# A Hymba-style decoder layer: part of the weight sums of its seven-product cells made by accumulating DMAs, and four more such cells

## The chip, the cores and the metric

The kernel runs on one core of a Trainium2 chip. A core has the matrix engine TensorE (PE; its weight loads are listed as PEld), VectorE (DVE), ScalarE (ACT), GpSimd (POOL) and SyncE (SP, which here only issues DMAs), and 16 DMA engines. The metric is the device time of one execution in microseconds (us), the median of several runs.

## The reference

One layer over 256 tokens with a model width of 2048, all in float32: RMSNorm and one input projection; a Mamba-2 style SSD scan and a sliding-window attention side by side; one output projection; a feed-forward block with a causal convolution over three tokens; and a gate that adds a per-layer embedding. The change lies in the last two parts:

```python
u = _rmsnorm(h, ffn_norm_g[i]) @ w_up[i]               # 2048 -> 2 * 5632
u = _causal_dwconv(u, ffn_conv_w[i], ffn_conv_b[i])
g_ff, u_ff = jnp.split(u, [D_FF], axis=-1)
h = h + (jax.nn.silu(g_ff) * u_ff) @ w_down[i]         # 5632 -> 2048
gate = jax.nn.sigmoid(_rmsnorm(h, ple_norm_g[i]) @ w_ple_gate[i])
pe = _rmsnorm(p[i] @ w_ple_proj[i], ple_post_g[i])
h = h + gate * pe
```

## The kernel before

**Products.** Each float32 operand is split into a rounded high part and a low part (`wh` by a cast on ACT, `wl` by a subtraction on DVE; the same for the left sides: `ah`, `al`, `ph`, `pl`, `gh`, `gl`). A product of a 128x128 block with a 128x512 block is three matmuls: high by high, high by low, low by high. They add up in one of eight PSUM banks. A weight load by SP brings 128 x 1024 values (512 KB), two blocks of 128x512; ACT casts the whole of it in one step and DVE subtracts the whole of it in one step.

**Cells.** The up projection runs over 11 pairs of columns `c` (512 gate columns and 512 value columns, loads `wg` and `wu`) and in each over eight slices of 256 input features, `kp`. One `kp` of one `c` is a cell: a 2x2 block matrix (two halves of the tokens, two halves of the features) by a 2x2 block matrix (two halves of the features, gate and value columns). A plain cell makes eight products. A mixed cell makes seven, after Winograd's form of Strassen's scheme: the left side is kept with four sums of its blocks (S1 to S4, made once, `left`), and on the weights' side four sums must be made anew in each cell. In `cell_mixed` they are a0, a1 (into a tile `ta`), b0 and b1 (written over `wg`), each a 128x512 step on DVE; then `ta` and the new `wg` are split like loaded weights, and the value half `wu[1]` is split by itself (`vh`, `vl`). A mixed cell's products go to banks P1, P6, P7, P5, which hold only mixed products and are combined by `sums` when the last mixed cell is through, and to Q2, Q4, Q3, Q22.

Which `kp` can be mixed is `MIXED`; which are, in a given `c`, is `FEWER`; the order of the cells is `BEGIN` for c = 0 and `STEADY` after it. The gate projection has the same cells in two passes (`GATES`, `GATES_SECOND`). There are 43 mixed cells: 2, 3, 3 in c = 0, 1, 2, four in each of c = 3 to 8, three in each of c = 9 and 10, and 3 + 2 in the gate passes.

**Stages.** After `up(c)` come the transposes, convolution and gating of its result (`gated`, which leaves `gh` and `gl` in one of `GBUF` buffers) and, from c = 2 on, two of the four output blocks of the down projection of the pairs finished before (`down`; four weight loads for each output block, two for each of the two pairs' `g`). The first output block's banks are P1 and P6 of the up stage just ended, the second's P7 and P5.

**Order.** Tiles are allocated in rings; a plan (`Plan`) holds every step with its engine, an assumed duration, what it follows and which ring slots it takes. PE's order is as written; the other engines' orders come from a list schedule by latest starts, in which `hop` is the time from one engine to another (0.15 us) and `lag` the time that a DMA needs beyond its issue. `QUEUE` is added to a hop in the first estimate of the latest starts. Each engine then works through its own list in order. Loads have a ring of `WR` = 7 raw buffers, splits a ring of `WB` + 1 = 5 pairs. For the two stages before (SSD and attention) `Recorder`, a subclass, does the same and may reorder PE too; it plans each of the two stages.

POOL does little in these stages: a power for each reciprocal root (line 664). It issues no DMA anywhere in the kernel.

Names that a reader of the profile meets: line 341 is the helper that all steps of the SSD and attention stages go through; 1511 and 1515 are the split of weights (ACT, DVE); 1557 to 1559 the three matmuls of a product; 1731 the sums b0 and b1, 1754 the sums a0 and a1, 1739 and 1743 the split of `vh`, `vl`; 1793 the sums out of the banks (`c<-c,b`); 1903 and 1907 the split of the gated block; 2104 to 2115 the gate's last steps and 2153 the last matmuls, of half width.

Of the kernel before, what the change touches and what calls it, by code (L numbers as in the profile page):

```python
# [21 lines left out]
P = 128  # L22
# [21 lines left out]
MIXED = (1, 3, 5, 7)  # L44
BEGIN = [0, 2, 4, 6, 1, 3, 5, 7]
STEADY = [0, 1, 2, 3, 5, 4, 7, 6]
FEWER = {0: (1, 3), 1: (1, 3, 5), 2: (1, 3, 5), 9: (1, 3, 5), 10: (1, 3, 5)}
GATES = (1, 3, 5)
GATE_FIRST = [0, 2, 1, 3, 4, 6, 5, 7]
GATES_SECOND = (3, 5)  # L50
AHEAD = 3
LEFT_DMA = (3,)
GATE_DMA = (1, 2)
QUEUE = 1.0
ROUNDS = 6
GBUF = 3
TAPS = (0,)
TURNED = ("xb", "xb", "xb", "xb")
KEYS_DMA = (True, True)
# [234 lines left out]
class Recorder(Plan):  # L294
# [29 lines left out]
    def keep(self, real, shape, pool=None, tag=None, n=1, at=-20.0, dtype=F32):  # L324
        t = Lazy(shape, dtype, None, real=real)
        t.at = at
        if pool is not None:
            t.slot = self.ring(pool, tag, n).take()
        return View.whole(t)

    def group(self, extra=0.0):
# [195 lines left out]
def hybrid_layer(  # L527
# [283 lines left out]
    rx = sb(const, [P, NB], "rx")  # L811
    dtT = sb(small, [64, T], "hsq")
    acc_b, acc_c = acc_pair(), acc_pair()
# [83 lines left out]
    def squares(ss, n):  # L897

        for b in range(NB):
            sq = sb(small, [P, NC], "hsq")  # L900
            S.activation(out=sq, in_=hres[b][:, n * NC : (n + 1) * NC], func=AF.Square, accum_out=ss[:, b, n : n + 1])
# [22 lines left out]
    with tc.tile_pool(name="ssd", bufs=1) as sp, tc.tile_pool(name="dram", bufs=1, space=bass.MemoryType.DRAM) as dp:  # L924
# [14 lines left out]
        dt_ps = plan.keep(dt_ps, [P, NC], ps_ms, "ms", 2, -5.0)  # L939
        dtT = plan.keep(dtT, [64, T], small, "hsq", 2)  # L940
        real_h, hres = hres, [plan.keep(t, [P, D]) for t in hres]
# [285 lines left out]
    with tc.tile_pool(name="att_s", bufs=2) as as_, tc.tile_pool(name="att", bufs=2, reuse_waits="tile") as ap_, tc.tile_pool(name="ps_sc", bufs=1, space=PSUM) as ps_sc:  # L1227
# [33 lines left out]
        def norm_rope(acc, b, rope, gain=None):  # L1261
            r = sb(ap_, [P, NC], "qkr")
            S.activation(out=r, in_=acc[b], func=AF.Copy, scale=rx[:, b : b + 1])
            n = sb(small, [P, NC], "hsq")
            S.activation(out=n, in_=r, func=AF.Square)
# [202 lines left out]
    pe_d = scratch.tile([NB, P, D], F32, tag="pe_d", name="pe_d")  # L1468
    by_hand = tc.manual_schedule(engines={PE.engine, S.engine, V.engine, nc.sync.engine})
    by_hand.__enter__()  # L1470

    with tc.tile_pool(name="ffn", bufs=2, reuse_waits="tile") as fp:

        plan = Plan(before.rest)
        UNIT = 0.2275
        raws = Ring(WR, [2.7 * i - 15.0 for i in range(WR)])
        splits = Ring(WB + 1, [-8.1, -5.4, -2.7, 0.0, 0.0])
        rings = {}
# [12 lines left out]
        def load(src):  # L1491
            o = Box()
            o.slot = raws.take()

            def go():
                o.t = load_raw(src)

            o.job = plan.add("SP", 2.0, go, slots=[o.slot], lag=2.2)
            return o

        def split_weights(src, after, slot):
            o = Box()
            o.slot = splits.take()
            pool = fp if o.slot[1] % (WB + 1) == WB else wp

            def tile_(t):
                return sb(pool, [P, KW, NC], t, F32R, 1 if pool is fp else None)

            def hi():
                o.h = tile_("wh")  # L1510
                S.copy(o.h, src.t)  # L1511

            def lo():
                o.l = tile_("wl")
                V.tensor_tensor(out=o.l, in0=src.t, in1=o.h.bitcast(F32), op=ALU.subtract)  # L1515

            a = plan.add("ACT", 1.0, hi, after, [o.slot])
            b = plan.add("DVE", 1.17, lo, [a, *after])
            free(slot, a, b)
            o.jobs = [a, b]  # L1520
            return o
# [146 lines left out]
        def left(o, kp, source, gains_, tiles):  # L1668
# [35 lines left out]
            prev = ins  # L1704
            for q, x0, x1, op in ((3, 7, 2, ALU.add), (4, 3, 0, ALU.subtract), (5, 0, 7, ALU.subtract), (6, 1, 4, ALU.subtract)):
                prev = [
                    plan.add("DVE", 0.22, lambda q=q, x0=x0, x1=x1, op=op: V.tensor_tensor(out=F.t[:, q, :], in0=F.t[:, x0, :], in1=F.t[:, x1, :], op=op), prev)
                ]
# [16 lines left out]

        def cell_mixed(acc, L, src):

            wg, wu = (load(x) for x in src)

            def into(x, i, y, j, z, k, op, after):  # L1730
                return plan.add("DVE", 0.61, lambda: V.tensor_tensor(out=x.t[:, i], in0=y.t[:, j], in1=z.t[:, k], op=op), after)

            g = split_weights(wg, [wg.job], wg.slot)
            v = Box()
            v.slot = ring("v")

            def v_hi():
                v.h = sb(fp, [P, NC], "vh", F32R, 1)
                S.copy(v.h, wu.t[:, 1])

            def v_lo():
                v.l = sb(fp, [P, NC], "vl", F32R, 1)
                V.tensor_tensor(out=v.l, in0=wu.t[:, 1], in1=v.h.bitcast(F32), op=ALU.subtract)

            vh = plan.add("ACT", 0.55, v_hi, [wu.job], [v.slot])
            vl = plan.add("DVE", 0.61, v_lo, [vh, wu.job])
            ta = Box()
            ta.slot = ring("ta")

            def sums(i, j, y, k):  # L1750

                def go():
                    t = alloc(ta, "t", lambda: sb(fp, [P, KW, NC], "ta", bufs=1))
                    V.tensor_tensor(out=t[:, i], in0=wu.t[:, j], in1=y.t[:, k], op=ALU.subtract)

                return plan.add("DVE", 0.61, go, [wu.job, y.job], [ta.slot])

            a0 = sums(0, 0, wg, 0)
            a1 = sums(1, 1, wu, 0)
            a = split_weights(ta, [a0, a1], ta.slot)  # L1760
            b0 = into(wg, 0, wu, 1, ta, 0, ALU.subtract, [a0, *g.jobs])
            b1 = into(wg, 1, wg, 1, wg, 0, ALU.subtract, [b0])
            b = split_weights(wg, [b0, b1], wg.slot)
            free(wu.slot, a0, a1, vh, vl, b0)
            free(ta.slot, b0)
            def at(f):
                return lambda: (L.h[:, f, :], L.l[:, f, :])

            ups = [(P1, A11, g, 0), (Q2, A12, g, 1), (Q3, S4, v, None), (P5, S1, a, 0), (P7, S3, a, 1), (P6, S2, b, 0), (Q4, A22, b, 1)]
            for o, jobs, n in ((g, g.jobs, 2), (v, [vh, vl], 1), (a, a.jobs, 2), (b, b.jobs, 2)):  # L1770
                parts = [
                    (acc[m], at(f), (lambda: (v.h, v.l)) if i is None else pick(o, i)) for m, f, x, i in ups if x is o
                ]
                free(o.slot, multiply(parts, jobs + L.jobs))

        def cell_plain(acc, L, src):

            for x, out_ in zip(src, ((Q2, Q4), (Q3, Q22))):
                w = weights(x)
                free(w.slot, multiply([(acc[m], block(L, i, b), pick(w, i)) for b, m in enumerate(out_) for i in range(KW)], w.jobs + L.jobs))  # L1780

        def sums(acc):
# [3 lines left out]
            u2 = sum_(x, c0, acc[P6], [j])  # L1786
            j1 = sum_(y, x, acc[P5], [u2])
            j2 = sum_(x, x, acc[P7], [u2, j1])
            j3 = sum_(z, x, acc[P5], [j2])
            return (c0, Q2, [j, u2]), (x, Q4, [j2, j3]), (y, Q3, [j1]), (z, Q22, [j3])  # L1790

        def sum_(out_, x, bank_, after=()):
            job = plan.add("DVE", 0.61, lambda: V.tensor_tensor(out=out_(), in0=x(), in1=bank_(), op=ALU.add), [bank_.last, *after], [out_.slot])
            free(bank_.slot, job)
# [120 lines left out]
        def up(c, at, order, mixed, before=None):  # L1915

            acc = accumulators(at, len(mixed))
            for n, kp in enumerate(order):
                if before:
                    before(n)  # L1920
                (cell_mixed if kp in mixed else cell_plain)(acc, lefts[kp], (w_up[c, kp], w_up[NPAIR + c, kp]))
                if n == max(order.index(m) for m in mixed):
                    rest = sums(acc)
# [27 lines left out]
        def square(ss, n, b, after=(), at=-20.0):  # L1951

            def go():
                sq = sb(small, [P, NC], "hsq")
                S.activation(out=sq, in_=hres[b][:, n * NC : (n + 1) * NC], func=AF.Square, accum_out=ss[:, b, n : n + 1])
# [106 lines left out]
        for n in range(4):  # L2062
            for b in range(NB):
# [6 lines left out]
                def square_pe(o=o, n=n, b=b):  # L2070
                    t = sb(small, [P, NC], "hsq")
                    S.activation(out=t, in_=o.t, func=AF.Square, accum_out=ssp[:, b, n : n + 1])
# [46 lines left out]
        def gate(first, at, order, mixed):  # L2119
            acc = accumulators(at, len(mixed))  # L2120
            last = order[-2:] if first else []
            if first:
                acc[Q22].left -= KW
            for n, kp in enumerate(order):
                if not first and n == 1:
                    if 3 not in GATE_DMA:
                        turn_h(3, (2, 3))
                if kp in last:
                    continue
                (cell_mixed if kp in mixed else cell_plain)(acc, gates[kp], (w_pg[first, kp], w_pg[first + 1, kp]))  # L2130
                if mixed and n == max(order.index(m) for m in mixed):
                    rest = sums(acc)
# [99 lines left out]
```

## Time and profile before

| | us |
|---|---|
| median of 3 runs | 1386.26 |
| lowest, highest | 1384.36, 1388.0 |
| the profiled execution's own time | 1385.08 |
| its span, from the first to the last instruction's end with its DMA | 1383.3 |

In the profile, busy times are sums over the span; a row of a group gives the line, the engine, the operation, what it writes and reads with the shapes, the count, then the busy time and the mean length in ns of one, then the engine's idle time just before them and what ended it. A row of the timeline gives the start, the length and the instruction. Lengths overlap: an engine starts a step before the one ahead of it has quite ended, so what a step costs an engine is the distance of two starts.

### The profile page before, as it was taken

Reading aid. Unit: us, or ns where it says so; the run is one execution under the profiler, and the core shown is the slowest. Engines: PE = TensorE matmul, PEld = TensorE weight load, DVE = VectorE, ACT = ScalarE, POOL = GpSimd, SP = SyncE. Lnnn points to the kernel's source line nnn. Section 1 sums busy time; section 2 is a strip of 40 time slices with the busy share of each in tenths; the row PEclk is TensorE's granted clock in tenths of the full one; section 3 lists DMA queues with packets and bytes.
Section 4 is the critical chain, followed back from the end, with each engine's and each line's share of the span. In section 5 each row is a group of like instructions: output and inputs, shape, how many; then the busy total and the mean of one; then the engine's idle time right before and its main releaser. Section 6 shows DMA issues by size and latency. Waiting matters only on the chain.

```text
span 1383.3 us, 18291 instructions
## 1 busy us (share of the span) xinstructions
PE 1374.8 (99%) x6302; PEld 1124.4 (81%) x6302; DVE 1208.3 (87%) x1581; ACT 1045.7 (76%) x1414; POOL 131.8 (10%) x113
## 2 busy tenths in 40 slices
PE   9999999999999999999999999999999999999998
PEld 7888888888777778888888888888888888888886
DVE  5788787776789898699999999999899999977998
ACT  6699988754677766587997896878688687867963
POOL 0001010037055421000000000000000000000000
PEclk9999999999999999999999999999999999999999
DMA  9888879868698778596868868686777678688762
GB/s 336 272 238 250 224 218 248 215 183 245 181 228 202 215 213 210 189 243 214 245 203 233 229 187 245 211 238 206 219 224 218 209 208 251 189 254 258 210 222 92
DMA packets 204220, 306.81 MB, mean 222 GB/s; under 512 B 129376, under 2 KB 134112, under 8 KB 203872
## 3 DMA queue, kind: packets, MB, share of 16 engines
q1 hardware_dynamic: 203696, 305.18, 76.2%
q8 instruction: 49, 0.80, 0.3%
q10 hardware_dynamic: 432, 0.48, 0.1%
q14 instruction: 43, 0.35, 0.1%
HBM read 271.46 MB, written 4.26 MB: 199 GB/s over the span
## 4 chain that ended last, share of the span: by engine, by line
PE 94%; DVE 3%; ACT 2%; issue 1%; DMA 0%; SPq 0%; DVEq 0%; ACTq 0%
PE acc L341 32%; PE b L1557 18%; PE b L1559 18%; PE b L1558 18%; PE acc L825 3%; PE ms L341 1%; PE sc L341 1%; DVE wl L1515 1%; PE tr L341 1%; ACT wh L341 1%; DMA seg<-scr 0%; PE ms L630 0%; DVE c L2115 0%; DVE c L2114 0%; PE b L1657 0%
## 5 line engine op out<-in xcount | busy, mean ns | idle before, releaser
L1511 ACT CAST wh<-w 128x1024 fp32r<-128x1024 f32 x296 | 308.3, 1051 | 128.5 <-PE b L1559 89.4
L1515 DVE TENSOR_TENSOR wl<-w,wh 128x1024 fp32r<-128x1024 f32 x296 | 355.9, 1220 | 38.1 <-ACT wh L1511 37.1
L341 DVE TENSOR_TENSOR wl<-w,wh 128x1024 fp32r<-128x1024 f32 x180 | 236.0, 1317 | 74.8 <-ACT wh L341 70.4
L341 ACT CAST wh<-w 128x1024 fp32r<-128x1024 f32 x180 | 188.1, 1049 | 128.1 <-PE acc L341 113.1
L341 PE MATMUL acc<-wh,ah 128*128 128x512 f32 x448 | 176.7, 394 | 0.0
L341 PE MATMUL acc<-wh,al 128*128 128x512 f32 x448 | 174.6, 390 | 0.0
L341 PE MATMUL acc<-wl,ah 128*128 128x512 f32 x448 | 174.4, 389 | 0.0
L1557 PE MATMUL b<-wh,gh 128*128 128x512 f32 x398 | 154.9, 389 | 0.0
L1559 PE MATMUL b<-wh,gl 128*128 128x512 f32 x398 | 154.8, 389 | 0.0
L1558 PE MATMUL b<-wl,gh 128*128 128x512 f32 x398 | 154.8, 389 | 0.0
L1559 PE MATMUL b<-wh,al 128*128 128x512 f32 x362 | 140.9, 389 | 0.0
L1557 PE MATMUL b<-wh,ph 128*128 128x512 f32 x352 | 137.1, 390 | 0.0
L1559 PE MATMUL b<-wh,pl 128*128 128x512 f32 x352 | 137.0, 389 | 0.0
L1558 PE MATMUL b<-wl,ph 128*128 128x512 f32 x352 | 136.9, 389 | 0.0
L1557 PE MATMUL b<-wh,ah 128*128 128x512 f32 x346 | 134.7, 389 | 0.0
L1558 PE MATMUL b<-wl,ah 128*128 128x512 f32 x346 | 134.7, 389 | 0.0
L341 PE MATMUL acc<-wh,yh 128*128 128x512 f32 x256 | 101.5, 396 | 0.0
L341 PE MATMUL acc<-wl,yh 128*128 128x512 f32 x256 | 99.8, 390 | 0.0
L341 PE MATMUL acc<-wh,yl 128*128 128x512 f32 x256 | 99.7, 389 | 0.0
L341 PEld LDWEIGHTS acc<-wh,ah 128*128 128x128 f32 x448 | 84.1, 188 | 18.7 <-issue 1.4
L341 PEld LDWEIGHTS acc<-wh,al 128*128 128x128 f32 x448 | 84.1, 188 | 17.7
L341 PEld LDWEIGHTS acc<-wl,ah 128*128 128x128 f32 x448 | 84.1, 188 | 17.1 <-issue 0.2
(292 smaller groups left out, 2518.3 us busy)
## 6 DMA issues: line engine op xcount, KB each, us to landing
w<-in_w_up_dram SPq DMA_DIRECT2D x176, 512.0 KB, 4.3
w<-in_w_in_dram SPq DMA_DIRECT2D x126, 512.0 KB, 4.3
w<-in_w_down_dram SPq DMA_DIRECT2D x88, 512.0 KB, 4.3
w<-in_w_out_dram SPq DMA_DIRECT2D x64, 512.0 KB, 4.4
w<-in_w_pg_dram SPq DMA_DIRECT2D x32, 512.0 KB, 4.2
seg<-scr SPq DMA_DIRECT2D x8, 512.0 KB, 5.3
xt<-in_xT_dram SPq DMA_DIRECT2D x16, 128.0 KB, 6.8
h<-in_x_dram SPq DMA_DIRECT2D x2, 1024.0 KB, 8.6
```

The source lines that it names most:

```text
L341: getattr(real, method)(*(concrete(a) for a in args), **{k: concrete(a) for k, a in kw.items()})
L825: PE.matmul(acc[b], lhsT=aT(k, b)[part % 2], rhs=wt[:, c, :], start=(k == 0 and not part), stop=(k == KT - 1 and part == 2))
L1511: S.copy(o.h, src.t)
L1515: V.tensor_tensor(out=o.l, in0=src.t, in1=o.h.bitcast(F32), op=ALU.subtract)
L1557: PE.matmul(t, lhsT=hi, rhs=wh, start=first, stop=False)
L1558: PE.matmul(t, lhsT=hi, rhs=wl, start=False, stop=False)
L1559: PE.matmul(t, lhsT=lo, rhs=wh, start=False, stop=last)
```

## The change

- Two of a mixed cell's four weight sums, a1 and b1, are made by DMAs issued on POOL that add a 128x512 block of SBUF (256 KB) onto another, in all cells but those of c = 0, and in the gate passes. For that the signs of left blocks and sums are turned so that all four weight sums are additions; `sums` subtracts in two places instead. The planner books 1.4 us on POOL and a lag of 3.4 us for such a DMA. POOL's order in these stages now comes from the plan too.
- What is split changes with it: a0 alone gets a narrow split (`vh`, `vl`), and the whole of `wu`, once a1 is added onto its first half, a wide one. A cell still has three wide and one narrow split.
- A mixed cell's last product pair (b) is put on PE's list after the first products of the next cell (`Between`, `later`, `DELAY`), and `sums` comes one cell later.
- Four more cells are mixed: one each in c = 1, 9 and 10, and one in the second gate pass; 47 in all. `STEADY` and `BEGIN` are reordered.
- One more raw buffer (`MORE`), one more split pair (`PAIRS`); `GBUF` goes from 3 to 2, the scratch tile `hsq` from two buffers to one, and `ta` is half as wide.
- In `Recorder`, a hop from another engine to PE counts 1 us more (`MARGIN`), so the SSD and the attention stage are planned anew; `QUEUE` goes from 1.0 to 0.5.

```diff
-BEGIN = [0, 2, 4, 6, 1, 3, 5, 7]
-STEADY = [0, 1, 2, 3, 5, 4, 7, 6]
-FEWER = {0: (1, 3), 1: (1, 3, 5), 2: (1, 3, 5), 9: (1, 3, 5), 10: (1, 3, 5)}
+BEGIN = [0, 2, 4, 1, 6, 3, 5, 7]
+STEADY = [1, 2, 0, 3, 5, 4, 7, 6]
+FEWER = {0: (1, 3), 1: (1, 3, 5, 7), 2: (1, 3, 5)}
-GATES_SECOND = (3, 5)
+GATES_SECOND = (1, 3, 5)
-QUEUE = 1.0
+QUEUE = 0.5
+MARGIN = 1.0
-GBUF = 3
+GBUF = 2
+BY_DMA = (('a1', 'b1'),)
+GATE_BY_DMA = ("a1", "b1")
+ADD_LAG = 3.4
+DELAY = 1
+MORE = 1
+PAIRS = 2
+TWICE = 1
...
+    def hop(self, a, b):
+        return super().hop(a, b) + (MARGIN if b.engine == "PE" and a.engine != "PE" else 0.0)
...
-            sq = sb(small, [P, NC], "hsq")
+            sq = sb(small, [P, NC], "hsq", bufs=1)
...
-        raws = Ring(WR, [2.7 * i - 15.0 for i in range(WR)])
-        splits = Ring(WB + 1, [-8.1, -5.4, -2.7, 0.0, 0.0])
+        raws = Ring(WR + MORE, [2.7 * i - 15.0 for i in range(WR + MORE)])
+        splits = Ring(WB + PAIRS, [-8.1, -5.4, -2.7, 0.0, *[0.0] * PAIRS])
...
+            def onto(name, x, i, y, k, after):
+                def go():
+                    if name in by_dma:
+                        G.dma_start(out=x.t[:, i], in_=y.t[:, k], accum_op=ALU.add)
+                    else:
+                        V.tensor_tensor(out=x.t[:, i], in0=x.t[:, i], in1=y.t[:, k], op=ALU.add)
+                if name in by_dma:
+                    return plan.add("POOL", 1.4, go, after, lag=ADD_LAG)
+                return plan.add("DVE", 0.61, go, after)
...
+            a0 = plan.add("DVE", 0.61, first, [wu.job, wg.job], [ta.slot])      # ta = wu[0] + wg[0]
+            ah = plan.add("ACT", 0.55, a_hi, [a0], [a.slot])
+            al = plan.add("DVE", 0.61, a_lo, [ah])
+            a1 = onto("a1", wu, 0, wu, 1, [a0])
...
+                b0 = plan.add(
+                    "DVE", 0.61, lambda: V.tensor_tensor(out=wg.t[:, 0], in0=wu.t[:, 1], in1=ta.t, op=ALU.add), [a0, *g.jobs]
+                )
+            b1 = onto("b1", wg, 1, wg, 0, [b0])
...
+            def later():
+                b = split_weights(wg, [b0, b1], wg.slot)
+                product(b, [(P6, S2, 0), (Q4, A22, 1)])
+
+            product(g, [(P1, A11, 0), (Q2, A12, 1)])
+            between()
+            product(a, [(P5, S1, None)])
+            v = split_weights(wu, [a1], wu.slot)
+            product(v, [(P7, S3, 0), (Q3, S4, 1)])
+            return later
...
-                if n == max(order.index(m) for m in mixed):
+                if n == len(order) - 1 or not DELAY:
+                    between()
+                if n == min(max(order.index(m) for m in mixed) + DELAY, len(order) - 1):
                     rest = sums(acc)
```

More of the change, by code (lines that the diff above doesn't have):

```diff
@@ L811, in hybrid_layer @@
     rx = sb(const, [P, NB], "rx")
-    dtT = sb(small, [64, T], "hsq")
+    dtT = sb(small, [64, T], "hsq", bufs=1)
     acc_b, acc_c = acc_pair(), acc_pair()
@@ L939, in hybrid_layer @@
         dt_ps = plan.keep(dt_ps, [P, NC], ps_ms, "ms", 2, -5.0)
-        dtT = plan.keep(dtT, [64, T], small, "hsq", 2)
+        dtT = plan.keep(dtT, [64, T], small, "hsq", 1)
         real_h, hres = hres, [plan.keep(t, [P, D]) for t in hres]
@@ L1263, in norm_rope @@
             S.activation(out=r, in_=acc[b], func=AF.Copy, scale=rx[:, b : b + 1])
-            n = sb(small, [P, NC], "hsq")
+            n = sb(small, [P, NC], "hsq", bufs=1)
             S.activation(out=n, in_=r, func=AF.Square)
@@ L1468, in hybrid_layer @@
     pe_d = scratch.tile([NB, P, D], F32, tag="pe_d", name="pe_d")
-    by_hand = tc.manual_schedule(engines={PE.engine, S.engine, V.engine, nc.sync.engine})
+    by_hand = tc.manual_schedule(engines={PE.engine, S.engine, V.engine, G.engine, nc.sync.engine})
     by_hand.__enter__()
@@ L1495, in go @@
             def go():
-                o.t = load_raw(src)
+                if o.slot[1] % (WR + MORE) == WR:
+                    o.t = sb(fp, [P, KW, NC], "w", bufs=1)
+                    nc.sync.dma_start(o.t, src)
+                else:
+                    o.t = load_raw(src)
             o.job = plan.add("SP", 2.0, go, slots=[o.slot], lag=2.2)
@@ L1503, in split_weights @@
             o.slot = splits.take()
-            pool = fp if o.slot[1] % (WB + 1) == WB else wp
+            pool = fp if o.slot[1] % (WB + PAIRS) >= WB else wp
             def tile_(t):
-                return sb(pool, [P, KW, NC], t, F32R, 1 if pool is fp else None)
+                return sb(pool, [P, KW, NC], t, F32R, PAIRS if pool is fp else None)
             def hi():
@@ L1704, in left @@
             prev = ins
-            for q, x0, x1, op in ((3, 7, 2, ALU.add), (4, 3, 0, ALU.subtract), (5, 0, 7, ALU.subtract), (6, 1, 4, ALU.subtract)):
+            for q, x0, x1, op in ((3, 7, 2, ALU.subtract), (4, 3, 0, ALU.subtract), (5, 0, 7, ALU.subtract), (6, 1, 4, ALU.add)):
                 prev = [
@@ L1724, in accumulators, with cell_mixed @@
             return [Bank(k, uses[m]) for m, k in enumerate(at)]
-        def cell_mixed(acc, L, src):
+        def cell_mixed(acc, L, src, between, by_dma=()):
             wg, wu = (load(x) for x in src)
-            def into(x, i, y, j, z, k, op, after):
-                return plan.add("DVE", 0.61, lambda: V.tensor_tensor(out=x.t[:, i], in0=y.t[:, j], in1=z.t[:, k], op=op), after)
-            g = split_weights(wg, [wg.job], wg.slot)
[L1734 to L1765, printed above, removed]
@@ new lines, in onto @@
+            def onto(name, x, i, y, k, after):
+                def go():
+                    if name in by_dma:
+                        G.dma_start(out=x.t[:, i], in_=y.t[:, k], accum_op=ALU.add)
+                    else:
+                        V.tensor_tensor(out=x.t[:, i], in0=x.t[:, i], in1=y.t[:, k], op=ALU.add)
+                if name in by_dma:
+                    return plan.add("POOL", 1.4, go, after, lag=ADD_LAG)
+                return plan.add("DVE", 0.61, go, after)
+            g = split_weights(wg, [wg.job], wg.slot)
@@ new lines, in cell_mixed, with first, a_hi, a_lo @@
+            ta, a = Box(), Box()
+            ta.slot, a.slot = ring("ta", TWICE), ring("v", TWICE)
+            def first():
+                ta.t = sb(fp, [P, NC], "ta", bufs=TWICE)
+                V.tensor_tensor(out=ta.t, in0=wu.t[:, 0], in1=wg.t[:, 0], op=ALU.add)
+            def a_hi():
+                a.h = sb(fp, [P, NC], "vh", F32R, TWICE)
+                S.copy(a.h, ta.t)
+            def a_lo():
+                a.l = sb(fp, [P, NC], "vl", F32R, TWICE)
+                V.tensor_tensor(out=a.l, in0=ta.t, in1=a.h.bitcast(F32), op=ALU.subtract)
@@ new lines, in cell_mixed @@
+            a0 = plan.add("DVE", 0.61, first, [wu.job, wg.job], [ta.slot])
+            ah = plan.add("ACT", 0.55, a_hi, [a0], [a.slot])
+            al = plan.add("DVE", 0.61, a_lo, [ah])
+            a.jobs = [ah, al]
+            a1 = onto("a1", wu, 0, wu, 1, [a0])
+            if "b0" in by_dma:
+                b0 = onto("b0", wg, 0, wu, 0, [a1, *g.jobs])
+            else:
+                b0 = plan.add(
+                    "DVE", 0.61, lambda: V.tensor_tensor(out=wg.t[:, 0], in0=wu.t[:, 1], in1=ta.t, op=ALU.add), [a0, *g.jobs]
+                )
@@ L1766, in at @@
+            b1 = onto("b1", wg, 1, wg, 0, [b0])
+            free(wu.slot, b0)
+            free(ta.slot, ah, al, b0)
             def at(f):
                 return lambda: (L.h[:, f, :], L.l[:, f, :])
[L1769 to L1774, printed above, removed]
@@ L1776, in cell_plain, with product @@
-        def cell_plain(acc, L, src):
+            def product(o, ups):
+                parts = [(acc[m], at(f), (lambda: (a.h, a.l)) if i is None else pick(o, i)) for m, f, i in ups]
+                free(o.slot, multiply(parts, o.jobs + L.jobs))
+            def later():
[4 more added lines that the diff above has]
+            product(a, [(P5, S1, None)])
@@ L1778, in cell_plain @@
+            v = split_weights(wu, [a1], wu.slot)
+            product(v, [(P7, S3, 0), (Q3, S4, 1)])
+            return later
+        def cell_plain(acc, L, src, between):
             for x, out_ in zip(src, ((Q2, Q4), (Q3, Q22))):
@@ L1780, in cell_plain, with nothing, __init__, __call__ @@
                 free(w.slot, multiply([(acc[m], block(L, i, b), pick(w, i)) for b, m in enumerate(out_) for i in range(KW)], w.jobs + L.jobs))
+                between()
+            return nothing
+        def nothing():
+            pass
+        class Between:
+            def __init__(self):
+                self.todo = nothing
+            def __call__(self):
+                do, self.todo = self.todo, nothing
+                do()
         def sums(acc):
@@ L1786, in sums, with sum_, go @@
             u2 = sum_(x, c0, acc[P6], [j])
-            j1 = sum_(y, x, acc[P5], [u2])
+            j1 = sum_(y, x, acc[P5], [u2], True)
             j2 = sum_(x, x, acc[P7], [u2, j1])
-            j3 = sum_(z, x, acc[P5], [j2])
+            j3 = sum_(z, x, acc[P5], [j2], True)
             return (c0, Q2, [j, u2]), (x, Q4, [j2, j3]), (y, Q3, [j1]), (z, Q22, [j3])
-        def sum_(out_, x, bank_, after=()):
-            job = plan.add("DVE", 0.61, lambda: V.tensor_tensor(out=out_(), in0=x(), in1=bank_(), op=ALU.add), [bank_.last, *after], [out_.slot])
+        def sum_(out_, x, bank_, after=(), less=False):
+            def go():
+                if less:
+                    V.tensor_tensor(out=out_(), in0=bank_(), in1=x(), op=ALU.subtract)
+                else:
+                    V.tensor_tensor(out=out_(), in0=x(), in1=bank_(), op=ALU.add)
+            job = plan.add("DVE", 0.61, go, [bank_.last, *after], [out_.slot])
             free(bank_.slot, job)
@@ L1917, in up @@
             acc = accumulators(at, len(mixed))
+            between = Between()
             for n, kp in enumerate(order):
@@ L1920, in up @@
                     before(n)
-                (cell_mixed if kp in mixed else cell_plain)(acc, lefts[kp], (w_up[c, kp], w_up[NPAIR + c, kp]))
-                if n == max(order.index(m) for m in mixed):
+                src = w_up[c, kp], w_up[NPAIR + c, kp]
+                if kp in mixed:
+                    between.todo = cell_mixed(acc, lefts[kp], src, between, BY_DMA[(c + mixed.index(kp)) % len(BY_DMA)] if c else ())
+                else:
+                    cell_plain(acc, lefts[kp], src, between)
+                if n == len(order) - 1 or not DELAY:
+                    between()
+                if n == min(max(order.index(m) for m in mixed) + DELAY, len(order) - 1):
                     rest = sums(acc)
@@ L1953, in go @@
             def go():
-                sq = sb(small, [P, NC], "hsq")
+                sq = sb(small, [P, NC], "hsq", bufs=1)
                 S.activation(out=sq, in_=hres[b][:, n * NC : (n + 1) * NC], func=AF.Square, accum_out=ss[:, b, n : n + 1])
@@ L2070, in square_pe @@
                 def square_pe(o=o, n=n, b=b):
-                    t = sb(small, [P, NC], "hsq")
+                    t = sb(small, [P, NC], "hsq", bufs=1)
                     S.activation(out=t, in_=o.t, func=AF.Square, accum_out=ssp[:, b, n : n + 1])
@@ L2121, in gate @@
             last = order[-2:] if first else []
+            summed = False
             if first:
                 acc[Q22].left -= KW
+            between = Between()
             for n, kp in enumerate(order):
@@ L2129, in gate @@
                     continue
-                (cell_mixed if kp in mixed else cell_plain)(acc, gates[kp], (w_pg[first, kp], w_pg[first + 1, kp]))
-                if mixed and n == max(order.index(m) for m in mixed):
+                src = w_pg[first, kp], w_pg[first + 1, kp]
+                if kp in mixed:
+                    between.todo = cell_mixed(acc, gates[kp], src, between, GATE_BY_DMA)
+                    if not DELAY or first and kp == [k for k in order if k not in last][-1] or n == len(order) - 1:
+                        between()
+                else:
+                    cell_plain(acc, gates[kp], src, between)
+                if mixed and between.todo is nothing and not summed and all(m in order[: n + 1] for m in mixed):
+                    summed = True
                     rest = sums(acc)
```

## Prediction

> **What bounds the kernel now.** I began with the page's engine lines and its chain, then asked for everything that TensorE (PE) ever waited for, then for the pace of single matmuls.
>
> ```profile
> PE 1374.8 (99%) x6302; PEld 1124.4 (81%) x6302; DVE 1208.3 (87%) x1581; ACT 1045.7 (76%) x1414; POOL 131.8 (10%) x113
> PE 94%; DVE 3%; ACT 2%; issue 1%; DMA 0%; SPq 0%; DVEq 0%; ACTq 0%
> ...
> PE ms L630 <- PEq L2222: 0.8, 1, 0.8
> PE ms L341 <- DVE uc L341: 0.8, 1, 0.8
> ```
>
> The first row alone proves little, since a pipelined matmul counts as busy. The last two rows are the whole answer of the view of waits for PE (total, times, longest): two waits, 1.6 us; asked from 600 us on, it is empty. The pace says the same:
>
> ```profile
> 707.12 0.39 PE L1559 MATMUL b<-wh,al 128*128 128x512 f32 x1
> ...
> 711.88 0.39 PE L1559 MATMUL b<-wh,pl 128*128 128x512 f32 x1
> ...
> 1376.20 0.28 PE L2153 MATMUL b<-wh,gl 128*128 128x256 f32 x1
> ```
>
> From the first to the second of these starts there are 21 steps in 4.76 us: 0.2267 us per 512-column matmul. The two windows of 62.5 us below each hold one up stage and one down stage, 180 and 96 matmuls: 276 x 0.2267 = 62.57 us of work against 62.5. Through the feed-forward and gate stages PE runs at its pace until its last matmul ends at 1376.5 (the third row). So time falls only by fewer matmuls, by the 1.6 us, or by the tail after 1376.5.
>
> ```profile
> 660.00:720.00 60.00, 60.00 (x265) 49.46 (x264) 58.36 (x74) 56.36 (x76) 0.00 (x0) 1.00 0.82 245
> ...
> 808.00:870.50 62.50, 62.50 (x277) 51.78 (x276) 60.32 (x75) 46.95 (x56) 0.00 (x0) 1.00 0.75 220
> 995.50:1058.00 62.50, 62.50 (x277) 51.75 (x276) 59.48 (x75) 51.72 (x65) 0.00 (x0) 1.00 0.73 217
> 1184.00:1225.50 41.50, 41.50 (x184) 34.35 (x183) 40.93 (x52) 30.25 (x37) 0.00 (x0) 1.00 0.65 213
> 1320.00:1376.50 56.50, 56.48 (x255) 46.80 (x253) 55.19 (x71) 28.70 (x32) 0.70 (x1) 1.00 0.44 142
> ```
>
> Columns: PE, PEld, DVE, ACT, POOL busy, granted clock (full), DMA share, GB/s. VectorE (DVE) is at 95-97% beside a PE that does not wait: a second engine just short of being the bound. ScalarE (ACT) has 11 to 16 us free in 62.5, only 3.6 between 660 and 720. POOL is empty.
>
> **The change part by part.** *Four more mixed cells* (one each at column pairs 1, 9, 10 and in the second gate pass). A mixed cell does 7 products where a plain one does 8, a product is three matmuls:
>
> ```profile
> L1557 PE MATMUL b<-vh,ah 128*128 128x512 f32 x43 | 16.7, 389 | 0.0
> L1754 DVE TENSOR_TENSOR ta<-w 128x512 f32<-128x512 f32 x43 | 29.4, 685 | 0.0
> L1731 DVE TENSOR_TENSOR w<-w 128x512 f32<-128x512 f32 x43 | 29.8, 692 | 1.4
> L1511 ACT CAST wh<-ta 128x1024 fp32r<-128x1024 f32 x43 | 45.2, 1051 | 19.9 <-PE b L1559 9.9 <-DVE ta L1754 8.6 <-ACT vh L1739 0.5
> L1739 ACT CAST vh<-w 128x512 fp32r<-128x512 f32 x43 | 26.5, 617 | 3.3 <-DMA w<-in_w_up_dram 3.3
> ...
> 853.76 0.68 DVE L1793 TENSOR_TENSOR c<-c,b 128x512 f32<-128x512 f32 x1
> 854.36 1.22 DVE L1515 TENSOR_TENSOR wl<-w,wh 128x1024 fp32r<-128x1024 f32 x1
> 855.49 0.68 DVE L1793 TENSOR_TENSOR c<-c,b 128x512 f32<-128x512 f32 x1
> ```
>
> 43 cells become 47; 4 x 3 x 0.2267 = 2.72 us off PE, all of it on the path. This is the one certain term.
>
> *DVE's share.* Started one behind another, a 512-wide step costs DVE 0.60 us and a 1024-wide one 1.13 (starts of the last three rows). A mixed cell now has three wide and five narrow steps, 6.4 us; with the sums a1 and b1 (the two DVE rows of lines 1754 and 1731) sent to DMAs it has three and three, 5.2. A plain cell has two wide, 2.3. All but the two cells of column pair 0 get DMAs: 41 old cells x 1.2 = 49 us off DVE, 4 new ones x 2.9 = 12 us on. A steady window goes from 60.3 to about 55.5. Worth nothing directly, PE being the bound; it is what lets the extra cells in. ACT still makes three wide casts and one narrow one per mixed cell, a plain cell two wide ones: each new cell adds 1.05 + 0.62 = 1.7 us. The tightest place is column pair 1, with 3.6 us free from 660 to 720: 0, while that holds.
>
> *The accumulating DMAs.* 90 of them, 256 KB each, issued by POOL. No trace row has a DMA from POOL or one that adds, so I bound it by transfers of that size and by what the engines carry (column: median us from issue to landing):
>
> ```profile
> q1 hardware_dynamic: 68571, 119.12, 74.7%
> w<-in_w_up_dram SPq DMA_DIRECT2D x129, 512.0 KB, 4.3
> ...
> pe_d<-c SPq DMA_DIRECT2D x8, 256.0 KB, 5.8
> out_dram<-c SPq DMA_DIRECT2D x7, 256.0 KB, 2.4
> ...
> 660.00:680.00 20.00, 20.00 (x90) 16.57 (x89) 19.73 (x24) 19.62 (x29) 0.00 (x0) 1.00 0.92 291
> 1330.00:1340.00 10.00, 10.00 (x46) 8.27 (x45) 9.54 (x12) 5.81 (x7) 0.00 (x0) 1.00 0.75 254
> ```
>
> Latency: 2.4 to 5.8 us, nearest to 5.8, since the engines are loaded. The kernel's planner books 1.4 on POOL plus 3.4 to landing, 4.8 us, inside these bounds; the price depends on how far the real one is from that (first rival). Engine load: the last row, where no transposes are under way, gives 7.5 us of engine time for 2.54 MB, so 0.262 MB is 0.77 us as a copy; read twice and written once, as an add must, at most 1.55. Eight per 62.5 us add 10 to 20% to the 74.7% of the first row (700 to 1240 us): 85 to 95%, at 255 to 290 GB/s. The row at 660 shows 0.92 and 291 GB/s for 20 us with PE at its pace, so I take no stall, with +9 us as the far end. By the Trainium skill (Collectives: The Full Stack, "The bandwidth ceiling") a reducing DMA makes two source reads and gets about half a copy's rate, so the sum would stand at the 95% end; no run here shows it yet. The Trainium skill (DMA: Bandwidth & Descriptors, "Issuing engines are not separate DMA queues") speaks against the change: POOL's transfers share the same 16 engines with the loads.
>
> *Queues.* POOL's other work in these stages is two tiny roots; the later one feeds the sigmoids, 16 us of cover if it stands behind a waiting DMA:
>
> ```profile
> 1324.97 0.70 POOL L664 TENSOR_TENSOR rg<-rs_t,nhalf 128x2 f32<-128x2 f32 x1 [55.10 <-DVE rs_t L662]
> ...
> 1340.73 1.95 ACT L2107 ACTIVATE c<-c,rg 128x512 f32<-128x512 f32 x3
> ```
>
> SP issues the same loads; a raw half now stays some 5 to 6 us longer (two per cell, four cells: about 50 us of buffer time per 62.5), which the one added raw buffer (62.5) repays. If that failed, loads would come late, and PE with them.
>
> *Two buffers for the gated block instead of three.* Column pair 4's block is written here, and the buffer that it must now share with pair 2 is last read at about 927.7:
>
> ```profile
> 926.15 1.04 ACT L1903 CAST gh<-cv 128x1024 fp32r<-128x1024 f32 x1
> 932.88 0.39 PE L1559 MATMUL b<-wh,gl 128*128 128x512 f32 x1
> 933.11 0.39 PE L1557 MATMUL b<-wh,ph 128*128 128x512 f32 x1
> 973.91 0.39 PE L1557 MATMUL b<-wh,gh 128*128 128x512 f32 x1
> ```
>
> The down stage ends at 933.1, its last two weight pairs (5.4 us) read the other block; so the write slips 1.5 us, and its reader comes at 973.9. Nothing.
>
> *Second half of a mixed cell delayed into the next cell, sums one cell later.* The down stage needs banks P1 and P6 at once. Now P6 is finished before the last plain cell:
>
> ```profile
> 968.24 0.39 PE L1559 MATMUL b<-wh,al 128*128 128x512 f32 x1
> 968.97 0.68 DVE L1793 TENSOR_TENSOR c<-c,b 128x512 f32<-128x512 f32 x1
> ```
>
> The sum that frees P6 ended 1.4 us after the mixed cell's last matmul began, and 24 more matmuls (5.4 us) stood before 973.9. After the change 12 stand there, 2.7 us. It fits with more than 1 us to spare if DVE comes at once. Cost: 0, up to 1.1 us (one wide step ahead of it) at each of nine borders, so up to 10 us.
>
> *Signs* change no instruction's shape: 0. *The margin* (1 us on each step that leads to PE, in the SSD and attention stages' plans) can win at most the 0.8 us wait on a record above; a worse order could cost a few us, as nothing hides a PE stall there. I take 0, ends -0.8 and +3.
>
> *The tail.*
>
> ```profile
> 1337.90 0.95 ACT wh L1511
> ...
> 1375.93 0.61 DVE c L2104
> ...
> 1376.56 1.52 ACT L2107 ACTIVATE c<-c,rg 128x512 f32<-128x512 f32 x3 [2.56 <-DVE c L2104]
> ...
> 1379.90 0.42 DVE c L2115
> ```
>
> From 1338 on the chain lies on DVE, beside PE. After the last matmul's end 6.8 us follow to the end of the span; the last sigmoid ends near 1378.1 and two 256-wide steps (0.84) would suffice behind it, where DVE takes till 1380.3: at most 1.4 us to win. The gate passes shed about 3 us of DVE work net (five cells at -1.2, one new at +2.9), all of it in the first pass, and PE shortens by 0.7 in the second. I take -0.5, ends -1.4 and +1.
>
> Sum: -2.7 -0.5 = -3.2 us. The profiled execution took 1385.1 (span 1383.3), 1.2 under the median of 1386.3; from the median, 1383.0.
>
> **The rivals.** *DMAs later than planned (slower).* The cast of the new wide half stands on ACT, in order, behind a1, and that of the last half behind b1; DVE's steps follow each. A lateness d over the 4.8 us is paid up to eight times per window. DVE will have 62.5 - 55.5 = 7 us free, so it decides from d of about 0.9 us; at 1.05 it is 8 x 1.05 - 7 = 1.4 us per window, 12 us over some 8.5 windows: 1395. For it: the 5.8 us row; against: full split buffers run ahead of PE, as this row (ACT waiting for PE to free them) shows.
>
> ```profile
> ACT wh L1511 <- PE b L1559: 99.3, 93, 1.7
> ```
>
> *P6 late at the borders.* Nine times 0.8 us: 1383 + 7 = 1390. For it: DVE in order; against: DVE gets freer. *DMA engines as the bound.* If an add cost three copies, 2.3 us each, the share would be 75 + 30 = 105%: 5% of 530 us, about 1410. Against: the page's stretches at over 290 GB/s. *A bit more than counted (faster).* The whole tail and the 0.8 us: -2.7 -1.4 -0.8 = -4.9, so 1381.4. *No effect on PE:* excluded, since the matmuls are gone; only waits can eat it.
>
> **How the numbers follow.** About 0.3% (4.2 us, 1382.1 to 1390.4) can be told from no change. Forecast 0.50 (its own range 1382 to 1386); the faster rival 0.23; late DMAs 0.14; borders 0.08 (about half of it within 0.3%); engines as the bound 0.05. So faster 0.23, same 0.54, slower 0.23. The range 1380.8 to 1395 leaves out the engine bound, half of the late DMAs and some of the faster end.
>
> **What would show it.** Right: 47 in the row of the narrow vh product; PE's list of waits still near 1.6 us; DVE near 55 us in a steady window; DMA share 0.85 to 0.95; an accumulating DMA landing within 5.7 us. Wrong: PE waiting for ACT or DVE on wh or wl (late DMAs), for DVE at c<-c,b where gh begins (borders), loads landing well beyond 4.3 us (engine bound), or new PE waits before 593 us (margin).

## The result and the profile after

The changed kernel takes 1404.9 us (median of 6 runs, 1401.5 to 1411.9) against 1385.9 (now also of 6 runs) for the kernel before: ratio 1.0145 (95% interval 1.0126 to 1.0164), 19 us slower, where 1383.0 was forecast and 1395 was the end of the range. Each later run's ratio is to runs of the kernel before made beside it (medians 1385.0 to 1385.5). The profiled execution took 1409.6, its span is 1407.9.

The page of the changed kernel, its engines, DMA queues, DMA issues, and PE's row for the narrow product:

```profile
PE 1381.1 (98%) x6290; PEld 1120.7 (80%) x6290; DVE 1174.4 (83%) x1515; ACT 1047.6 (74%) x1422; POOL 210.5 (15%) x203
...
q1 hardware_dynamic: 203696, 305.18, 73.9%
q0 software_dynamic: 12960, 23.60, 9.9%
...
w<-in_w_up_dram SPq DMA_DIRECT2D x176, 512.0 KB, 4.8
w<-w POOLq DMA_DIRECT2D x90, 256.0 KB, 5.6
...
L1572 PE MATMUL b<-vh,ah 128*128 128x512 f32 x47 | 19.6, 418 | 8.3 <-DVE h L2003 4.4 <-ACT vh L1767 2.6 <-DVE c L1842 1.2
```

There are 47 mixed cells and 12 matmuls fewer, DVE is 34 us less busy, and yet PE is later:

```profile
1016.95 0.39 PE L1572 MATMUL b<-wh,ah 128*128 128x512 f32 x1
...
1400.70 0.28 PE L2220 MATMUL b<-wh,gl 128*128 128x256 f32 x1
```

The last matmul starts at 1400.70 instead of 1376.20: 24.5 us later with 2.7 us less to do, so PE lost 27.2 us. From that start to the end of the span it takes as long as before (7.2 us, 7.1 before), so nothing was lost in the tail. The busy share tells nothing (98% for 99%). PE's whole list of waits, which held two entries before:

```profile
PE b L1572 <- DVE c L1842: 7.3, 8, 1.6
PE b L1572 <- DVE h L2003: 4.4, 6, 1.3
PE b L1572 <- ACT vh L1767: 2.6, 2, 1.8
PE b L1573 <- DVE vl L1771: 2.6, 4, 1.0
PE ms L641 <- PEq L2289: 0.9, 1, 0.9
PE acc L836 <- ACT wh L680: 0.8, 1, 0.8
PE b L1573 <- DVE wl L1530: 0.6, 2, 0.3
PE b L1574 <- DVE gl L1958: 0.6, 1, 0.6
```

The list counts only idle time beyond a matmul's modelled end, so it sums to less than 27; from 600 us on, the distances of starts beyond 0.2267 add up to 27.6. Behind PE, in the waits of the other engines:

```profile
DVE wl L1530 <- ACT wh L1526: 87.6, 76, 5.7
ACT wh L1526 <- DMA w<-w: 60.7, 30, 5.4
```

In the kernel before, DVE's wait for the same step was

```profile
DVE wl L1515 <- ACT wh L1511: 37.4, 41, 2.1
```

ACT stood 60.7 us behind accumulating DMAs, and DVE, which takes over from ACT, 87.6 (37.4 before). One case in order of time, from the timelines of POOL, ACT, DVE and PE (start, length, instruction, idle time before it and what ended it):

```profile
760.97 1.77 POOL L1749 DMA_DIRECT2D w<-w  x2 [6.62 <-DVE w L1782]
765.97 0.87 POOL L1749 DMA_DIRECT2D w<-w  x1 [3.23 <-DMA w<-in_w_up_dram]
...
770.03 1.05 ACT L1526 CAST wh<-w 128x1024 fp32r<-128x1024 f32 x1 [3.23 <-DMA w<-w]
771.11 1.23 DVE L1530 TENSOR_TENSOR wl<-w,wh 128x1024 fp32r<-128x1024 f32 x1 [5.68 <-ACT wh L1526]
...
775.88 1.04 ACT L1526 CAST wh<-w 128x1024 fp32r<-128x1024 f32 x1 [0.92 <-DMA w<-w]
776.83 0.61 ACT L1767 CAST vh<-ta 128x512 fp32r<-128x512 f32 x1
777.50 0.49 PE L1572 MATMUL b<-vh,ah 128*128 128x512 f32 x1 [1.82 <-ACT vh L1767]
```

The add issued at 760.97 (the first of that row's two) landed about 9.0 us later, that of 765.97 9.8 us later, where the plan has 4.8. The cast at 775.88 waits for the second; `vh` at 776.83 needs no DMA at all, but stands behind it in ACT's order, and PE, which had come to that product at 775.5, waits for `vh`. ACT has idle time enough on the whole (26% of the span); it is the order that passes the delay on. The wait also cost more than itself: in the 3.5 us from 779.7 on the granted clock is 0.51, and seven matmuls start 0.43 us apart instead of 0.23, another 1.4 us.

The second kind of loss is at the borders of the stages, here at the start of an up stage:

```profile
1017.64 1.23 DVE L1530 TENSOR_TENSOR wl<-w,wh 128x1024 fp32r<-128x1024 f32 x1 [1.75 <-ACT wh L1526]
1018.78 1.27 DVE L2003 TENSOR_TENSOR h<-h,b 128x512 f32<-128x512 f32 x2
...
1018.09 0.39 PE L1574 MATMUL b<-wh,al 128*128 128x512 f32 x1
1019.52 0.50 PE L1572 MATMUL b<-vh,ah 128*128 128x512 f32 x1 [1.04 <-DVE h L2003]
```

The new `STEADY` starts with a mixed cell. Six matmuls (1.4 us) after the down stage's end PE wants bank P5 for the `vh` product, and P5 still holds the down stage's result: DVE empties it at 1018.78, late because a weight step before it had waited for ACT. Nothing was late in the same place before, where a plain cell of 24 matmuls stood first. By the distances of starts, some 16 of the 27.6 us lie at the borders of stages, the rest inside them.

### The profile page after: what moved, and what is told of

Same layout as the page of the kernel before. It is cut to its first block, busy times and chain, and to the rows that moved or that the text cites. A ratio compares the mean times of both kernels' runs of the same rounds, so it can differ in the third digit from the quotient of the medians.

```text
span 1407.9 us, 18590 instructions
## 1 busy us (share of the span) xinstructions
PE 1381.1 (98%) x6290; PEld 1120.7 (80%) x6290; DVE 1174.4 (83%) x1515; ACT 1047.6 (74%) x1422; POOL 210.5 (15%) x203
## 3 DMA queue, kind: packets, MB, share of 16 engines
q0 software_dynamic: 12960, 23.60, 9.9%
## 5 line engine op out<-in xcount | busy, mean ns | idle before, releaser
L1530 DVE TENSOR_TENSOR wl<-w,wh 128x1024 fp32r<-128x1024 f32 x343 | 412.2, 1220 | 89.0 <-ACT wh L1526 87.6
L1526 ACT CAST wh<-w 128x1024 fp32r<-128x1024 f32 x343 | 352.7, 1048 | 141.5 <-DMA w<-w 60.7
L352 DVE TENSOR_TENSOR wl<-w,wh 128x1024 fp32r<-128x1024 f32 x180 | 237.1, 1325 | 79.4 <-ACT wh L352 77.0
L352 ACT CAST wh<-w 128x1024 fp32r<-128x1024 f32 x180 | 187.3, 1049 | 114.5 <-PE acc L352 104.1
L1749 POOL DMA_DIRECT2D w<-w x90 | 78.8, 907 | 653.0 <-DVE ta L1763 350.9
```

Source lines behind the costliest of these rows:

```text
L352: getattr(real, method)(*(concrete(a) for a in args), **{k: concrete(a) for k, a in kw.items()})
L1749: G.dma_start(out=x.t[:, i], in_=y.t[:, k], accum_op=ALU.add)
```

## The experiments

Two theories. **Lateness:** adds land later than the plan says, and ACT and DVE, working in order, pass it on. **Order:** a stage that starts with a mixed cell, and sums that come one cell later, leave DVE no time at the borders, whatever the DMAs do.

**The order alone put back.**

```diff
-STEADY = [1, 2, 0, 3, 5, 4, 7, 6]
+STEADY = [0, 1, 2, 3, 5, 4, 7, 6]
```

> The changed kernel with one line put back: STEADY starts with the plain cell 0 again ([0,1,2,3,5,4,7,6]), so a stage's first mixed product stands 24 matmuls (5.4 us) behind the border and not at it. Order theory (a stage that begins with a mixed cell needs at once banks that DVE is still emptying: P5 after a down stage, P1 and P5 after column pairs 0 and 1): the PE waits at the starts of the up stages, 6.6 us after a down stage and 4.8 us at pairs 1 and 2, go: about 1405 - 11 = 1394. Late-DMA theory (ACT and DVE wait in order for adds that land later than planned): at most 3 us, 1402 or more.

Measured: 1396.2, ratio 1.0073 (1.0058 to 1.0088). Nearly 9 us back, where lateness alone would have let at most 3 go. The waits for `h` are gone from PE's list, those for `c<-c,b` fall from 7.3 to 0.8, but the ones for `vh` and `vl` stay:

```profile
PE b L1572 <- ACT vh L1767: 2.7, 3, 2.2
PE b L1573 <- DVE vl L1771: 1.9, 3, 0.8
...
PE b L1572 <- DVE c L1842: 0.8, 1, 0.8
```

So the order is a real part, and not the whole.

**The adds back on DVE, the rest as changed.**

```diff
-BY_DMA = (('a1', 'b1'),)
-GATE_BY_DMA = ("a1", "b1")
+BY_DMA = ((),)
+GATE_BY_DMA = ()
```

> The changed kernel with all four weight sums on DVE again (no accumulating DMA anywhere), everything else kept, 47 mixed cells too. Late-DMA theory: ACT's 61 us of waiting for adds and the 8 us that PE waits for vh, vl, wl inside stages go; DVE goes from 88% back to about 97% of a steady window: 1405 - 8 = 1397, or less if border waits are late DVE work too. Order theory: the 17 us of waits at borders stay or grow, since DVE is fuller: 1400 to 1410.

Measured: 1389.7, ratio 1.0030 (1.0018 to 1.0042): better than expected by 7 us, since most border waits went too, with the order untouched. DVE was late at the borders because it had waited for ACT. DVE's wait for ACT fell from 87.6 us to 20.1. A steady window shows a PE at its pace with DVE at 96% (63 us are 278 steps of 0.2267):

```profile
825.00:888.00 63.00, 63.00 (x279) 52.18 (x278) 60.56 (x76) 46.95 (x58) 0.00 (x0) 1.00 0.76 215
```

DVE needs no relief there. What is left is some 5 us of PE's time at pairs 1 and 2 and the down stage after them, nearly all before 751 us, and the tail: the last matmul starts at 1377.57 and the span ends at 1388.1, 10.5 us where it was 7.1.

**The same slow adds, but planned for.**

```diff
-ADD_LAG = 3.4
+ADD_LAG = 6.0
```

> The changed kernel, its planner told that an add lands 6.0 us after POOL is done instead of 3.4 (measured from the issue: mean 5.7, nine in ten within 7.6; planned 4.8, now 7.4). The adds stay as slow as they are, only the orders of ACT and DVE change. Late-DMA theory: ACT's wait for adds falls from 61 us to under 15, and PE's waits inside stages (8 us) with it: about 1397. If the time does not move, lateness against the plan is not what costs.

Measured: 1389.5, ratio 1.0033 (1.0018 to 1.0047), 15 us back by one number in a planner; the adds land no sooner (mean 6.1 us, 5.7 before). ACT's wait for them is halved, not under the 15 us expected. The time still went below the 1397 expected, since waits at the borders fell with it:

```profile
ACT wh L1526 <- DMA w<-w: 28.1, 19, 2.5
```

This run also settles the rival of the DMA engines as the bound. From 700 to 1240 us their share was 0.94 (0.91 as changed), weight loads of the up stage landed in 5.1 us (4.8), and yet PE was busy for 538.4 of these 540 us (527.0).

**Both edits**, the order put back and the lag at 6.0 (the first and the third diff).

> The changed kernel with both edits at once: STEADY starts with plain cell 0, and the planner is told 6.0 us of lag. With the lag alone the waits at the starts of pairs 1 and 2 (3.7 us) are what is left of the order's part; if the two causes are separate, they go: 1389.5 - 3.7 = about 1386. If a late plan only hid behind the order, no better than 1389.

Measured: 1387.3, ratio 1.0014 (1.0005 to 1.0023). That is short of the 1386 expected of two separate causes. The order alone was worth 9, the lag 15, both 17.6. They overlap: the tight borders cost mainly when DVE comes late, and the late adds are what made it late.

**No adds and the old order** (the first and the second diff).

> The changed kernel without accumulating DMAs and with STEADY starting with plain cell 0. Order theory: of the 5.6 us that PE still waited without DMAs, the 3.0 at stage starts go: 1389.7 - 3 = about 1386.5; the tail, 10.3 us after the last matmul where the kernel before has 6.8, stays, since DVE has all the sums of six gate cells. Adds needed theory (DVE too full without them): no gain.

Measured: 1387.4, ratio 1.0017 (1.0008 to 1.0026). That is 2.4 us better, near the 3 expected by the order theory; the tail is still 9.3 us.

**Copies in the place of adds** (the DMAs overwrite a1's and b1's target instead of adding to it, so those two sums are left out).

```diff
-G.dma_start(out=x.t[:, i], in_=y.t[:, k], accum_op=ALU.add)
+G.dma_start(out=x.t[:, i], in_=y.t[:, k])
```

> The changed kernel with its 90 DMAs as plain copies of the same 256 KB to the same place: the addition in a1 and b1 is left out, so the sums are not made. Two-reads theory (a 2 KB packet of an add takes 178 ns, a plain one 84): copies land in about 4.6 us instead of 5.7, under the planner's 4.8; ACT's wait for them falls under 20 us and the time to about 1393 (orders' part stays). If the issue from POOL or the queueing is what is slow, landing and time stay near 5.5 us and 1403.

Measured: 1385.0, ratio 1.0000 (0.9991 to 1.0009). Everything but the adding is as changed: 90 DMAs, their waits, POOL's queue, the plan and the order. The 20 us by which it is below the changed kernel are the whole loss against the kernel before, and more than the 12 expected.

```profile
q0 software_dynamic: 7200, 23.60, 4.6%
w<-w POOLq DMA_DIRECT2D x90, 256.0 KB, 3.8
ACT wh L1526 <- DMA w<-w: 11.5, 6, 2.6
L1749 POOL DMA_DIRECT2D w<-w x90 | 49.3, 549 | 655.6 <-DVE ta L1763 228.7 <-ACT wh L1526 173.0 <-DVE w L1782 148.0
```

For the same bytes the adds took 9.9% of 16 engines over 1407.9 us, the copies 4.6% of 1383.2: 1.55 us of engine time for one add, 0.71 for one copy. The Trainium skill (Collectives: The Full Stack, "The bandwidth ceiling") has a reducing DMA at about half a copy's rate for its second source read; the ratio here is near it, 2.2 times. That the second read is the cause, no run here shows: the adds also went in smaller packets (12960 for the same 23.60 MB, the copies 7200). An add is also longer on POOL (0.91 us for 0.55), and lands in 5.6 us for 3.8. 76 of the 90 copies landed within the plan's 4.8, 29 of the 90 adds. Engine time, time on POOL and landing all fell together here; the run with the lag of 6.0, where the adds were as costly as ever, shows that the plan's error is the larger part.

**The margin and `QUEUE` alone**, on the kernel before.

```diff
-QUEUE = 1.0
+QUEUE = 0.5
+MARGIN = 1.0
+    def hop(self, a, b):
+        return super().hop(a, b) + (MARGIN if b.engine == "PE" and a.engine != "PE" else 0.0)
```

> The kernel before with only the planner's margin (1 us on hops to PE in the SSD and attention stages) and QUEUE 0.5. The changed kernel enters the feed-forward part 1.1 us earlier than the one before: expected 0 to -1.5 us, 1384.5 to 1386; were it slower by over 2 us, the margin or QUEUE would carry a part of the loss.

Measured: 1383.8, ratio 0.9985 (0.9976 to 0.9995): a small gain, a little above the 0 to 1.5 us expected. It is no part of the loss.

**The four more cells on the kernel before**, with the margin and every sum on DVE.

```diff
-FEWER = {0: (1, 3), 1: (1, 3, 5), 2: (1, 3, 5), 9: (1, 3, 5), 10: (1, 3, 5)}
+FEWER = {0: (1, 3), 1: (1, 3, 5, 7), 2: (1, 3, 5)}
-GATES_SECOND = (3, 5)
+GATES_SECOND = (1, 3, 5)
```

> The kernel before with the margin, QUEUE 0.5 and the four more mixed cells, all sums on DVE in the old way, old orders and buffers. If DVE can carry them: 1383.8 - 2.7 = 1381. If it is too full: PE waits at pairs 1, 9 or 10 or a longer tail (as without DMAs, +3.5), 1383 to 1388; that would show what the DMAs were for.

Measured: 1388.6, ratio 1.0027 (1.0017 to 1.0036). Here DVE is too full, at two places: the tail is 10.6 us (span 1386.9, last matmul at 1376.30), and from 699 to 731, in pair 2's stage and at the start of the first down stage behind it, where ACT is full too:

```profile
699.00:731.00 32.00, 29.36 (x127) 23.30 (x125) 31.62 (x44) 31.66 (x43) 0.00 (x0) 1.00 0.67 200
```

DVE and ACT are at 99% and PE, at 29.4 of 32, waits. These waits follow from pair 1's fourth cell: with three cells there, in the next run, PE is busy for all of the 32 us.

**Only the two cells at pairs 9 and 10**, again with the margin.

```diff
-FEWER = {0: (1, 3), 1: (1, 3, 5), 2: (1, 3, 5), 9: (1, 3, 5), 10: (1, 3, 5)}
+FEWER = {0: (1, 3), 1: (1, 3, 5), 2: (1, 3, 5)}
```

> The kernel before with the margin, QUEUE 0.5 and mixed cells added only at column pairs 9 and 10 (45 in all), no accumulating DMAs. If the loss of the 47-cell form without DMAs lies at pair 1 (4.5 us of PE waits from 699 to 731 us) and in the gate's tail (10.3 us after the last matmul), both go: 1383.8 - 4 x 0.68 / 2 = 1382.4, under both kernels. If DVE is too full at pairs 9 and 10: 1384 or more.

Measured: 1382.4, ratio 0.9979 (0.9971 to 0.9988): the expected number, and the lowest time of all. PE keeps its pace through both pairs with DVE at 97%:

```profile
1164.00:1226.00 62.00, 62.00 (x275) 51.32 (x275) 60.19 (x75) 49.53 (x60) 0.00 (x0) 1.00 0.75 214
```

**Fewer adds**, three runs with the lag of 6.0, the old order and three mixed cells at pair 1 (46 in all): adds in the gate passes only (12), all of them (88; the expectation says 84), and a1 alone in the up stages (50).

```diff
-FEWER = {0: (1, 3), 1: (1, 3, 5, 7), 2: (1, 3, 5)}
+FEWER = {0: (1, 3), 1: (1, 3, 5), 2: (1, 3, 5)}
-BY_DMA = (('a1', 'b1'),)
+BY_DMA = ((),)            # the first; unchanged in the second; (('a1',),) in the third
```

> The changed kernel with DMA adds in the gate passes only (12 of 90), 6.0 us of lag, STEADY starting with plain cell 0, three mixed cells at pair 1 (46 in all). Without adds in the up stages no wait in order there; at the tail the adds take DVE's excess away: PE without waits, tail 7 us: about 1382. If the adds at the gate cost what they cost elsewhere: about 1384; if the tail stays at 9 to 10 us: 1385.

> All 84 remaining adds by DMA, 6.0 us of lag, STEADY starting with plain cell 0, three mixed cells at pair 1 (46): against the same with four there (1387.3), the 2.5 us of waits between 700 and 731 us go and 0.7 us of matmuls come back: 1385.5. If those waits are the adds' and not the cell's: 1388.

> As the one with 46 cells and 6.0 us of lag, but in the up stages only a1 is added by DMA, b1 stays on DVE: half the doubled packets. Load theory (the adds' engine time itself delays loads and other adds): waits shrink by about half of what is left, 1384. Lateness in order alone, already planned for: no difference to the run with both, 1385.5.

Measured: 1383.7, ratio 0.9989 (0.9980 to 0.9998); 1385.6, ratio 1.0000 (0.9991 to 1.0009); 1383.2, ratio 0.9984 (0.9974 to 0.9993). The fourth cell at pair 1 had cost 1.6 us net. 50 adds are 2.4 us better than 88 though both are planned with the same lag: a planned lag does not make them free (b1's step came back to DVE, which had room). The load theory expected such a gain, but the adds that were left landed hardly sooner (median 5.1 us for 5.2), so whether load or the mere number of late adds made it stays open. With 12 adds PE's tail is back at 7.1 us (last matmul 1374.47, span 1381.6), but one wait of 1 us in the second gate pass eats the cell's 0.7: the third gate cell pays nothing either way.

## Why the prediction was wrong

- *Four cells, 2.72 us:* right as far as it goes; at pairs 9 and 10, with nothing else in the way, two cells brought 1383.8 to 1382.4, the 1.4 us of their matmuls, though the intervals of the two ratios overlap. "0, while that holds" for pair 1 was wrong: ACT's 3.6 free us of the window from 660 to 720 did not hold from 699 to 731. The right question was what the engines have free where the stage's first gated block is due, not over a window of 60.
- *The adds, "no stall":* the step that failed most. The engine time was bounded well (0.77 to 1.55 us; 1.55). The latency was bounded by median rows (2.4 to 5.8; median 5.6), and the rival of late DMAs was priced with one lateness d for all: 5.7 - 4.8 = 0.9 us, just at its threshold. The threshold itself was wrong. It set DVE's 7 us of free time in a window against the lateness, but free time at another moment does not pay for a wait in order: here DVE is idle for 9.6 of 65 us, and PE is not busy for 1.8.

```profile
887.00:952.00 65.00, 63.21 (x277) 51.27 (x276) 55.35 (x66) 49.22 (x62) 6.99 (x8) 1.00 0.92 245
```

  With the order put back the adds came 0.5 us late in the mean, well under the threshold, and still the run took some 8 us more than with the lag of 6.0 (ratios 1.0073 and 1.0014). The spread is a part of it: in this execution one add in ten took more than 7.6 us, the longest 9.8, and an early one gives nothing back. But of ACT's 60.7 us only some 17 ended with the landing of one of these. Other waits are longer than their add was late (4.1 us, behind one that landed in 5.5), so a late issue or the order itself is in them; no run parts the two. Whatever stops ACT stops DVE and then PE. The row that I held against it, ACT waiting for PE with full buffers (99.3 us), fell to 53.6.
- *The reordered cells:* `STEADY` beginning with a mixed cell was not costed at all. Put back, it gave 9 us while adds were late and 2 once they were planned for or gone. I priced a border at nine times 0.8 us as a rival, but only the one at the start of the down stage (P6). That one happened too, at four of its starts: 3.5 of the 7.3 us of waits for `c<-c,b`; the other 3.8 lie at the starts of pairs 1 and 2.
- *Relief of DVE lets the cells in:* right for the tail, where without it 3.4 us are lost, wrong for the steady windows, where PE kept its pace with all sums on DVE. The 78 adds of the up stages bought nothing that a run shows.
- *Two gated buffers, raw buffers, POOL's roots, signs:* taken at 0. With copies, all of these were in place and the time was that of the kernel before, so together they cost no more than the some 4 us that the cells and the margin should have brought; they were not tried apart, and the trace puts most of these 4 us elsewhere (below).
- *Margin:* 0 with an end at -0.8; with `QUEUE` and on the kernel before it gave 1.7 (0.15%).
- *Tail:* -0.5; it came out as before, 7.2 us.

Of its signs of being right, the 47 cells, DVE's share, the DMA share (0.88 to 0.92) and the median landing of an add (5.6) all came, and the time was wrong all the same: none of them tells what an engine that works in order stands behind. PE's list of waits did.

With copies, PE still lost 3.6 us from 600 us on by the distances of its starts: some 2.3 at the starts of pairs 1 and 2, where the new order was still in place, and 0.8 before `gl` near 730, a wait that the run with 47 cells and the old buffers has too. So little is left for the gated and raw buffers. What stays open is what the 38 or 78 adds of the up stages still cost once they are planned for (2.4 us from 88 to 50): their load on the engines, or their number.

## What to carry to other kernels

Where PE already runs without a wait, an edit that frees another engine is worth only the matmuls that it lets you drop; count those first, and here they were 2.7 us. Work moved from an engine to a DMA turns a fixed duration into one with a spread, and engines that work in order pay for the late end of it: do not plan with the median of the landing times (here 7.4 us, near the slow tenth of 7.6, in the place of 4.8 gave 15 us back; no other lag was tried), and put nothing that does not need the DMA behind the step that does. Before reordering a stage, ask of its first product which bank it needs and who empties it.

## What was new about the hardware

An accumulating DMA within SBUF cost 2.2 times a copy's engine time (1.55 us of all 16 engines for 0.71 per 256 KB), 1.65 times on POOL (0.91 us for 0.55), and 1.8 us more to land (5.6 for 3.8), with the loads' queue at some 74% of the engines. Beside 90 of them, weight loads of the up stage took 4.8 us instead of 4.3. DVE ran at 96 to 97% beside a PE that did not wait, where nothing that it followed came late (60.19 of 62 us). After two of PE's longest waits the granted clock fell to half for some 3.4 us: 0.51 in the 3.5 us from 779.7 on, after a stretch of 4.5 us in which PE was busy for 1.8, and 0.51 from 665.5 to 669.0 with the order put back, after 1.5 of 4.6.
